# A single-core hybrid attention block: earlier weights for head 1, and low parts moved from GpSimd to VectorE

## The chip, the cores and the metric

The kernel runs on one core of a Trainium2 chip. The metric is the device time of one launch in microseconds (us). Three runs of the kernel before took 897.99, 901.11 and 902.21 us, with a median of 901.11 us. All times below come from one further execution, which the hardware profiler recorded.

## What is computed

One layer of a hybrid encoder block works on 1024 tokens of width 1024, in float32. The input is normed, multiplied by one wide matrix `w_in`, and the columns of the result go to a gated linear attention with four heads and to a short gated convolution. Both are gated, joined, and sent through `w_out`. The reference, cut to what matters here:

```python
h = rmsnorm(x, norm_g)                        # x * rsqrt(mean(x*x) + eps) * g
proj = jnp.einsum('bsd,de->bse', h, w_in)     # 1024 x 1024 by 1024 x 7200
q, k, v, z_a, lr_f, lr_b, b_gate, c_gate, h_c, z_c = split(proj)
o = gla(q, k, v, decay(lr_f)) + reversed_gla(q, k, v, decay(lr_b))
y_a = rmsnorm(o) * gla_norm_g * silu(z_a)
y_c = b_gate * conv3(c_gate * h_c) * silu(z_c)
out = rmsnorm(x + concat(y_a, y_c) @ w_out, final_g)
```

Only the columns of `v` and the preparation of `h` for the later columns are touched by the change.

## The kernel before, in words

**Split numbers.** TensorE multiplies in a reduced float32 format. Each operand is kept as two tiles: a high part `hi` (a cast of the number) and a low part `lo` (the number less its high part). A product is three matmuls, hi by hi, hi by lo and lo by hi. The helper `split` (L150 to L153) makes the two: ScalarE casts, and GpSimd subtracts unless another engine is named.

**The x stage (L214 to L265).** The eight tiles of 128 tokens are loaded, scaled by their root mean square and by `norm_g` (spread over the partitions into the tile `gb` by two matmuls), transposed on TensorE, and split into the blocks `hb`. Between these steps TensorE multiplies the tiles that are ready by the weights of head 0's values, one block `t` per tile. All of this is in an order written out by hand (`tc.manual_schedule`), and so is the next stage. Head 1's weights are loaded in block 4 and split after block 7, in whole tiles of 128x1024.

**The values of head 1 (L285 to L344).** `values(1, wv)` runs 192 matmuls in four steps. Beside each step, `sums` prepares a quarter of three sums of the blocks of `h`, called t1, t2 and t3. They are needed later, since a product of two 2x2 block matrices is made with seven block products instead of eight. Each sum is a subtraction on VectorE (L310) and a split: a cast on ScalarE (`t_hi`) and a subtraction on GpSimd (`t_lo`).

**The values of heads 2 and 3 (`value_pair`, L453).** Seven block products, each in two halves, with weights a00, a01, a10, a11 and sums of them. In the order of TensorE: o00, o01, os2 (with t2), os3 (with t3), os1 (with t1), o11 (with t4) and os4. VectorE adds each result from its PSUM bank (L483 to L502). Beside o01, os2 and os3 it runs the generator `later_sums`, which makes a fourth sum t4 and three sums of quarter blocks (tt1, tt2, tt3). Six banks (pa, pb, pc, twice each) are used in turn, so product 15 waits until VectorE has taken product 9 from its bank.

**The pairs of columns (`quad`, L544).** All further columns go through `second` (products of quarter blocks) and `pair` (products of blocks). The first `quad` begins where `value_pair` ends; its first bank is that of os1. `second` adds its second product to the first at L528, and TensorE then reuses that bank.

**What sets the order.** Each engine takes its own instructions in order, and engines wait for each other on semaphores. Where no order is written out, a scheduler places the instructions, and `issue_after` pins some of them. All loads and stores go through the one queue of the sync engine, also in order.

Of the kernel before, what the change touches and what calls it, by code (L numbers as in the profile page):

```python
# [37 lines left out]
def tile_hybrid_gla_shortconv(ctx, tc, x, norm_g, w_in, w_gk_f, b_gk_f, w_gk_b, b_gk_b,  # L38
# [66 lines left out]
    ident = const.tile([P, P], F32, name="ident")  # L105
    make_identity(nc, ident)
    ones = xp.tile([1, P], F32, name="ones")
    G.memset(ones, 1.0)
    mhalf = const.tile([P, 1], F32, name="mhalf")
    G.memset(mhalf, -0.5)  # L110
    smask = const.tile([P, 512], F32, name="smask")
# [62 lines left out]
    def scale_x(t, rs):  # L174
        for o in (0, 512):
            sl = slice(o, o + 512)
            V.scalar_tensor_tensor(xts[t][:, sl], xts[t][:, sl], rs, gb[:, sl], ALU.mult, ALU.mult)  # L177

    def turn_x(t):

        for d in range(2):
            ps = pq.tile([P, 512], F32, name=("pa", "pb", "pc")[(2 * t + d) % 3])
            for c in range(4):
                T.transpose(ps[:, c * P:(c + 1) * P], xts[t][:, (4 * d + c) * P:(4 * d + c + 1) * P], ident)
            hi, lo = (b[:, :, t % 4 * P:(t % 4 + 1) * P] for b in hb[d][t // 4])
# [4 lines left out]
    def h_tile(part, c, t):  # L190
        return hb[c // 4][t // 4][part][:, c % 4, t % 4 * P:(t % 4 + 1) * P]

    def split_v(raw, e_hi=A, e_lo=G):
        pr = tuple(vw.tile([P, 4, DV], F32R, name=f"v_{n}") for n in ("hi", "lo"))
        split(*pr, raw, e_hi, e_lo)
        return pr

    last_mm = [None]

# [13 lines left out]

    with tc.manual_schedule():  # L214

        gb = xp.tile([P, D], F32, name="gb")

        def spread_g(o, scaled):
            ps = bank()
            T.matmul(ps, ones, g_row[:, o:o + 512], start=True, stop=True)  # L220
            scaled(gb[:, o:o + 512], ps)

        spread_g(0, lambda dst, src: V.tensor_scalar(dst, src, D ** 0.5, None, ALU.mult))
        rs0 = scale_of(0)
        spread_g(512, lambda dst, src: A.activation(dst, src, AF.Copy, scale=D ** 0.5))
        scale_x(0, rs0)
# [10 lines left out]
        src = lr_w.rearrange("p c (d k) -> p c d k", d=2)  # L240

        def split_lr(r):
            split(lrw6[:, :, :, r, 0], lrw6[:, :, :, r, 1], src, V, G)

        for t in range(NT):
            ps = bank()[:, 0:DV]
            mul_v(ps, t, wv, 0)
            if t + 2 < NT:
                rs = scale_of(t + 2)
            if t == 0:  # L250
                mul_v(ps, t, wv, 1)
            if t + 1 < NT:
                turn_x(t + 1)
            if t + 2 < NT:
                scale_x(t + 2, rs)
            if t > 0:
                mul_v(ps, t, wv, 1)
            mul_v(ps, t, wv, 2)
            store_v(0, t, ps)
            if t == NT - 4:  # L260
                raws = [load_v(1, i) for i in range(2)]
            if t in (4, 5):
                split_lr(t - 4)
            if t == NT - 1:
                w_next = [split_v(r) for r in raws]  # L265
    wv = w_next
    gk_hi, gk_lo = (fl(a) for a in y_pair())
    split(gk_hi, gk_lo, gk, V, V)
# [25 lines left out]


    t1, t2, t3 = (block(tp, f"t{i}") for i in (1, 2, 3))
    raws = [load_v(h, i) for h in (2, 3) for i in range(2)]

    def f_tile():
        return gt.tile([P, 512], F32, name="f")  # L300
# [5 lines left out]

    done = []

    def minus(a, b_, blk, c, f):
        done.append(V.tensor_tensor(f, a, b_, ALU.subtract))  # L310
        split(blk[0][:, c], blk[1][:, c], f)

    def sums():
        for c in range(4):
            f01, f00, f11 = (joined(hb[d][s_], c) for d, s_ in ((0, 1), (0, 0), (1, 1)))
            minus(f01, f00, t1, c, f00)
            minus(f11, f01, t3, c, f01)
            minus(f11, f00, t2, c, f11)
# [5 lines left out]
    def less(f, x, y, blk):  # L324
        V.tensor_tensor(f, x, y, ALU.subtract)
        split(*blk, f)


    quarters = [tuple(a[:, 2 * d:2 * d + 2, 256 * s_:256 * s_ + 256] for a in hb[1][0])
# [4 lines left out]
    def part(src, e_lo=G, late=False):  # L334
        pool, name, bufs = (resp, "w", 2) if late else (ws, "a", 6)
        hi, lo = (pool.tile([P, 4, P], F32R, name=f"{name}_{i}", bufs=bufs) for i in ("hi", "lo"))
        hi, lo = (a[:, 0:src.shape[1]] for a in (hi, lo))
        split(hi, lo, src, A, e_lo)
        return hi, lo
# [6 lines left out]
    def halves(a):  # L346
        return [a[:, o:o + 4] for o in (0, 4)]

    def parts(a):
        return [part(x) for x in halves(a)]  # L350

    a00, a01, a10, a11 = (fl(r).rearrange("p (c e) -> p c e", e=P) for r in raws)
    o00, o01 = parts(a00), parts(a01)
# [99 lines left out]
    def value_pair(h0, h1, o00, o01, os2, a00, a01, a10, a11, s2, beside):  # L453
# [24 lines left out]
        x, w = [tmp(), tmp()], [None, None]  # L478
        for i, ps in mul(o00, b00):
            A.copy(x[i], ps)  # L480
        for i, ps in mul(o01, b10):
            c = tmp()
            V.tensor_tensor(c, ps, x[i], ALU.add)  # L483
            out_v(h0, 0, i, c)
            next(beside)
        for i, ps in mul(os2, t2):
            V.tensor_tensor(x[i], ps, x[i], ALU.add)
            next(beside)
        for i, ps in mul(os3, t3):
            w[i] = tmp()  # L490
            V.tensor_tensor(w[i], ps, x[i], ALU.add)
            next(beside)
        for i, ps in mul(os1, t1):
            c = tmp()
            V.tensor_tensor(c, ps, w[i], ALU.add)
# [148 lines left out]

    def later_sums():

        for c in range(4):
            f = joined(t2, c, tmp)
            minus(joined(hb[1][0], c, tmp), f, t4, c, f)
            yield  # L650
        f = [tmp().rearrange("p (c t) -> p c t", c=2) for _ in range(3)]
        for f_, i in zip(f, (0, 1, 3)):
            whole(f_, quarters[i])
        less(f[0], f[1], f[0], tt1)
        yield
        less(f[1], f[2], f[1], tt3)
        less(f[0], f[2], f[0], tt2)
        yield

    with tc.issue_after(last_mm[0].ins):  # L660
# [4 lines left out]
    less(f[0], f[1], f[0], quarters[1])  # L665
    h2 = quarters[0], tt1, tt2, tt3, quarters[2], quarters[3], quarters[1]

    for j in range(CW // P):
# [380 lines left out]
```

## Time and profile before

| quantity | value |
|---|---|
| median of three runs | 901.11 us (897.99 to 902.21) |
| profiled execution, whole | 903.29 us |
| its span, first to last instruction | 901.2 us |
| TensorE (PE) busy | 865.7 us, 96% |
| VectorE (DVE) busy | 713.4 us, 79% |
| GpSimd (POOL) busy | 448.2 us, 50% |
| ScalarE (ACT) busy | 393.7 us, 44% |
| mean granted TensorE clock | 0.986 of full speed |

The span is what the trace covers; the profiled execution's own time has 2.1 us around it. A busy share is an average over stages that differ much: VectorE is at 79% overall and at almost 100% in some stretches of the first 130 us. TensorE's granted clock is 1.00 (2.4 GHz) or 0.50 (1.2 GHz) at any moment; a value between is the mean of a window. In a timeline an instruction's bracket tells how long its engine stood idle before it, and which instruction released it.

### The profile page before, as it was taken

The page shows a single profiled execution, that of the slowest core. Times are in us where ns is not written, and L with a number is a line of the kernel's source. Part 1 is how long each engine was busy: PE and PEld are TensorE (multiplying, and loading weights), DVE is VectorE, ACT ScalarE, POOL GpSimd, SP SyncE. Part 2 cuts the span into 40 slices and gives each one's busy share as a digit, 9 for nine tenths or more (in the row PEclk, how much of TensorE's full clock was granted, in tenths as well). Part 3 has the DMA queues.
Part 4 walks back from the last instruction along what each step waited for, and adds up shares of the span by engine and source line. Part 5 has one row for each costly group of instructions (what it writes and reads, how often), then busy time and mean ns, then how long its engine had stood idle before and what let it go on. Part 6 is the DMA issues. An engine that isn't in the chain of part 4 may idle for free.

```text
span 901.2 us, 12971 instructions
## 1 busy us (share of the span) xinstructions
PE 865.7 (96%) x4452; PEld 725.2 (80%) x4452; DVE 713.4 (79%) x1283; ACT 393.7 (44%) x822; POOL 448.2 (50%) x391
## 2 busy tenths in 40 slices
PE   7999969999999999999999999999999999999996
PEld 6999958887887878787878888887878787888885
DVE  6879986888888888888888565666799989975754
ACT  5533233434445362635344342443365446542553
POOL 3368676757768576768665655520112212222231
PEclk9999969999999999999999999999999999999999
DMA  7521332222231313132233433468856344310122
GB/s 252 138 74 56 86 109 56 71 70 71 71 94 48 117 47 105 60 94 71 70 94 129 134 102 116 128 208 327 293 159 222 105 136 134 120 52 24 42 77 93
DMA packets 102163, 100.35 MB, mean 111 GB/s; under 512 B 10705, under 2 KB 82385, under 8 KB 101586
## 3 DMA queue, kind: packets, MB, share of 16 engines
q1 hardware_dynamic: 102098, 99.53, 35.0%
q8 instruction: 35, 0.57, 0.3%
q14 instruction: 30, 0.25, 0.1%
HBM read 71.20 MB, written 28.31 MB: 110 GB/s over the span
## 4 chain that ended last, share of the span: by engine, by line
PE 72%; DVE 17%; issue 4%; DMA 3%; POOL 2%; ACT 1%; SPq 0%; POOLq 0%; DVEq 0%; ACTq 0%
PE out L715 16%; PE pc L381 15%; PE pb L381 15%; PE pa L381 15%; PE po L872 3%; PE pu L917 2%; DVE tmp L304 1%; DVE tmp L635 1%; DVE tmp L430 1%; DVE f L304 1%; DMA k<-k_dram 1%; DVE s L407 1%; DMA raw<-in_w_in 1%; DVE xt L177 1%; DVE dd L820 1%
## 5 line engine op out<-in xcount | busy, mean ns | idle before, releaser
L153 POOL TENSOR_TENSOR a_lo<-s,a_hi 128x512 fp32r<-128x512 f32 x74 | 116.0, 1573 | 28.8 <-ACT a_hi L152 28.5
L153 POOL TENSOR_TENSOR a_lo<-tmp,a_hi 128x512 fp32r<-128x512 f32 x48 | 70.3, 1466 | 103.8 <-ACT a_hi L152 99.0
L153 POOL TENSOR_TENSOR a_lo<-raw,a_hi 128x512 fp32r<-128x512 f32 x84 | 111.2, 1327 | 14.8 <-ACT a_hi L152 14.8
L147 POOL TENSOR_TENSOR rs<-rs,mhalf 128x1 f32<-128x1 f32 x48 | 28.7, 598 | 142.6 <-DVE rs L146 135.2
L715 PE MATMUL out<-a_hi,y_hi 128*128 128x512 f32 x192 | 89.2, 465 | 0.5 <-ACT y_hi L152 0.5
L152 ACT CAST a_hi<-raw 128x512 fp32r<-128x512 f32 x108 | 63.8, 595 | 58.3 <-PE pc L381 17.2
L152 ACT CAST a_hi<-tmp 128x512 fp32r<-128x512 f32 x48 | 29.8, 621 | 122.8 <-DVE tmp L407 99.4
L715 PE MATMUL out<-a_hi,y_lo 128*128 128x512 f32 x192 | 77.1, 401 | 0.0
L715 PE MATMUL out<-a_lo,y_hi 128*128 128x512 f32 x192 | 77.0, 401 | 0.0
L827 POOL TENSOR_TENSOR kt<-kt,k 128x256 f32<-128x256 f32 x32 | 26.3, 821 | 97.7 <-ACT kt L824 70.8
L152 ACT CAST a_hi<-s 128x512 fp32r<-128x512 f32 x74 | 45.0, 617 | 47.4 <-PE pa L381 17.5
L381 PE MATMUL pa<-h_hi,a_hi 128*128 128x512 f32 (+1 forms) x128 | 47.7, 373 | 5.2 <-DVE tmp L528 2.8
L381 PE MATMUL pb<-h_hi,a_hi 128*128 128x512 f32 (+1 forms) x128 | 48.2, 376 | 4.5 <-DVE tmp L528 3.8
L381 PE MATMUL pc<-h_hi,a_hi 128*128 128x512 f32 (+1 forms) x128 | 48.0, 375 | 2.6 <-DVE tmp L528 2.6
L381 PE MATMUL pa<-h_hi,a_lo 128*128 128x512 f32 (+1 forms) x128 | 47.0, 367 | 0.7 <-POOL a_lo L153 0.7
L381 PE MATMUL pc<-h_lo,a_hi 128*128 128x512 f32 (+1 forms) x128 | 47.2, 369 | 0.0
L381 PE MATMUL pb<-h_hi,a_lo 128*128 128x512 f32 (+1 forms) x128 | 47.2, 369 | 0.0
L381 PE MATMUL pc<-h_hi,a_lo 128*128 128x512 f32 (+1 forms) x128 | 47.1, 368 | 0.0
L381 PE MATMUL pb<-h_lo,a_hi 128*128 128x512 f32 (+1 forms) x128 | 47.1, 368 | 0.0
L381 PE MATMUL pa<-h_lo,a_hi 128*128 128x512 f32 (+1 forms) x128 | 46.8, 365 | 0.0
L715 PEld LDWEIGHTS out<-a_hi,y_lo 128*128 128x128 f32 x192 | 36.4, 190 | 8.0
L717 DVE TENSOR_TENSOR res<-out,res 128x512 f32<-128x512 f32 x48 | 32.9, 686 | 12.4 <-PE out L715 12.3
(344 smaller groups left out, 2735.2 us busy)
## 6 DMA issues: line engine op xcount, KB each, us to landing
raw<-in_w_in SPq DMA_DIRECT2D x56, 512.0 KB, 4.0
raw<-in_w_out SPq DMA_DIRECT2D x16, 512.0 KB, 3.9
xt<-in_x SPq DMA_DIRECT2D x8, 512.0 KB, 8.4
yc_dram<-tmp SPq DMA_DIRECT2D x16, 256.0 KB, 2.0
b_dram<-u SPq DMA_DIRECT2D x8, 512.0 KB, 2.6
z_dram<-tmp SPq DMA_DIRECT2D x16, 256.0 KB, 2.4
s<-yc_dram SPq DMA_DIRECT2D x16, 256.0 KB, 3.9
raw<-in_x SPq DMA_DIRECT2D x8, 512.0 KB, 6.7
```

What stands on the lines that cost most here:

```text
L147: G.tensor_tensor(rs, rs, mhalf, ALU.pow)
L152: (e_hi.copy if e_hi is A else e_hi.tensor_copy)(hi, src)
L153: e_lo.tensor_tensor(lo, src, hi.bitcast(F32), ALU.subtract)
L177: V.scalar_tensor_tensor(xts[t][:, sl], xts[t][:, sl], rs, gb[:, sl], ALU.mult, ALU.mult)
L304: V.tensor_tensor(f, blk[0].bitcast(F32)[:, c], blk[1].bitcast(F32)[:, c], ALU.add)
L381: T.matmul(ps, a[x0][:, k], b_[x1][:, k], start=start and k == 0 and j == 0, stop=stop and k == n - 1 and j == 2, skip_group_check=not start)
L407: V.tensor_tensor(f, x0, x1, op)
L715: T.matmul(ps, a[:, j, :], w, start=j == 0 and i == 0, stop=j == 3 and i == 2)
L717: V.tensor_tensor(res[t][:, cs], ps, (xr if row0 == NT else res[t])[:, cs], ALU.add)
L827: G.tensor_tensor(kk, kk, k4, ALU.mult)
L872: T.matmul(o, l, m, start=j == 0, stop=j == len(mm) - 1)
L917: T.matmul(pu[:, d], ks[:, d], r["v"][:, t], start=True, stop=True)
```

## The change

- Head 1's two weight tiles are loaded directly behind the eight tiles of x, and are split in halves of 128x512 after blocks 5 and 6. The loads of a00 and a01 move up to block 1, those of a10 and a11 to block 6; o00 is split at block 7.
- `gb` stays in the PSUM tiles `pc`; the factor D ** 0.5 goes into the row of ones. The two copies of it are gone, and `turn_x` takes only the banks pa and pb.
- The low parts of t1, t2, t3 (12 subtractions), of t4 (4) and of tt1, tt2, tt3 (3) go from GpSimd to VectorE, and are written behind the next sum instead of at once. The last quarter (`quarters[1]`) keeps its split on GpSimd.
- `later_sums` gives t4 in two steps, beside the two halves of the first product, and its further steps beside the second.

```diff
+    v_raw1 = [load_v(1, i) for i in range(2)]      # behind load_x(2..7)
     ...
-    G.memset(ones, 1.0)
+    G.memset(ones, D ** 0.5)
     ...
-            V.scalar_tensor_tensor(xts[t][:, sl], xts[t][:, sl], rs, gb[:, sl], ALU.mult, ALU.mult)
+            V.scalar_tensor_tensor(xts[t][:, sl], xts[t][:, sl], rs, gb[o // 512], ALU.mult, ALU.mult)
     ...
-            ps = pq.tile([P, 512], F32, name=("pa", "pb", "pc")[(2 * t + d) % 3])
+            ps = pq.tile([P, 512], F32, name=("pa", "pb")[d])
     ...
-        split(*pr, raw, e_hi, e_lo)
+        for o in (0, 2):
+            split(*(a[:, o:o + 2] for a in (*pr, raw)))
     ...
+        gb = [pq.tile([P, 512], F32, name="pc") for _ in range(2)]
+        for i in range(2):
+            T.matmul(gb[i], ones, g_row[:, 512 * i:512 * i + 512], start=True, stop=True)
     ...
-            if t == NT - 4:
-                raws = [load_v(1, i) for i in range(2)]
+            if t == 1:
+                a00, a01 = (load_a(2, i) for i in range(2))
+            if t in (5, 6):
+                w_next.append(split_v(v_raw1[t - 5]))
+            if t == 6:
+                a10, a11 = (load_a(3, i) for i in range(2))
     ...
-            if t == NT - 1:
-                w_next = [split_v(r) for r in raws]
+            if t == 7:
+                o00 = parts(a00)
     ...
-    def minus(a, b_, blk, c, f):
+    def split_later(behind, hi, lo, f):
+
+        A.copy(hi, f)
+        for x in behind:
+            V.tensor_tensor(*x, ALU.subtract)
+        behind[:] = [(lo, f, hi.bitcast(F32))]
+
+    def finish_low(behind):
+        while behind:
+            V.tensor_tensor(*behind.pop(), ALU.subtract)
+
+    def minus(a, b_, blk, c, f, behind):
         done.append(V.tensor_tensor(f, a, b_, ALU.subtract))
-        split(blk[0][:, c], blk[1][:, c], f)
+        split_later(behind, blk[0][:, c], blk[1][:, c], f)
     ...
         for i, ps in mul(o00, b00):
             A.copy(x[i], ps)
+            next(beside)
         for i, ps in mul(o01, b10):
     ...
             next(beside)
         for i, ps in mul(os2, t2):
             V.tensor_tensor(x[i], ps, x[i], ALU.add)
-            next(beside)
         for i, ps in mul(os3, t3):
             w[i] = tmp()
             V.tensor_tensor(w[i], ps, x[i], ALU.add)
-            next(beside)
     ...
-            minus(joined(hb[1][0], c, tmp), f, t4, c, f)
-            yield
+            minus(joined(hb[1][0], c, tmp), f, t4, c, f, behind)
+            if c % 2 == 1:
+                yield
+        finish_low(behind)
     ...
-        less(f[0], f[1], f[0], tt1)
+        less(f[0], f[1], f[0], tt1, behind)
         yield
-        less(f[1], f[2], f[1], tt3)
-        less(f[0], f[2], f[0], tt2)
+        less(f[1], f[2], f[1], tt3, behind)
+        less(f[0], f[2], f[0], tt2, behind)
+        finish_low(behind)
         yield
```

The first place is VectorE beside the values of head 1, from the last tile of x on. `f` holds a sum of two parts (L304; L320 in the changed kernel) or a difference of two sums (L310; L337), `t_lo` is a low part, and the rows with `out` belong to the decay's low-rank input. Before:

```order
L304 TENSOR_TENSOR f<-h_hi,h_lo 128x512 x3
L310 TENSOR_TENSOR f<-f 128x512 x3
L304 TENSOR_TENSOR f<-h_hi,h_lo 128x512
L278 TENSOR_TENSOR y_hi<-out,y_hi 32x512 x2
L278 TENSOR_TENSOR y_lo<-out,y_lo 32x512 x2
L304 TENSOR_TENSOR f<-h_hi,h_lo 128x512 x2
L310 TENSOR_TENSOR f<-f 128x512 x3
L304 TENSOR_TENSOR f<-h_hi,h_lo 128x512
```

In the changed kernel the same place reads:

```order
L320 TENSOR_TENSOR f<-h_hi,h_lo 128x512 x3
L337 TENSOR_TENSOR f<-f 128x512 x2
L295 TENSOR_TENSOR y_hi<-out,y_hi 32x512 x2
L295 TENSOR_TENSOR y_lo<-out,y_lo 32x512 x2
L329 TENSOR_TENSOR t_lo<-f,t_hi 128x512
L337 TENSOR_TENSOR f<-f 128x512
L329 TENSOR_TENSOR t_lo<-f,t_hi 128x512
L334 TENSOR_TENSOR t_lo<-f,t_hi 128x512
L320 TENSOR_TENSOR f<-h_hi,h_lo 128x512 x3
L337 TENSOR_TENSOR f<-f 128x512 x2
```

Each quarter of the sums now has three more subtractions on VectorE, each behind the next difference, and the third directly behind the second.

The second place is GpSimd from the last block of the x stage on. `v_lo` is head 1's low part, `a_lo` that of the weights (from `raw` as loaded, or from their sums in `s`), `t_lo`, `h_lo`, `y_lo` and `tt_lo` those of t1 to t3, t4, tt1, and tt2 with tt3. Before:

```order
L153 TENSOR_TENSOR a_lo<-raw,a_hi 128x512 x4
L153 TENSOR_TENSOR v_lo<-raw,v_hi 128x1024 x2
L153 TENSOR_TENSOR t_lo<-f,t_hi 128x512 x12
L603 MEMSET u 128x1
L604 MEMSET u 128x1
L153 TENSOR_TENSOR a_lo<-s,a_hi 128x512 x2
L153 TENSOR_TENSOR a_lo<-raw,a_hi 128x512 x3
L153 TENSOR_TENSOR h_lo<-tmp,h_hi 128x512
...
L153 TENSOR_TENSOR a_lo<-raw,a_hi 128x512 x2
L153 TENSOR_TENSOR y_lo<-tmp,y_hi 128x512
L153 TENSOR_TENSOR tt_lo<-tmp,tt_hi 128x512 x2
```

In the changed kernel:

```order
L154 TENSOR_TENSOR v_lo<-raw,v_hi 128x512 x2
L154 TENSOR_TENSOR lrw<-lr_w,lrw 128x16x16
L154 TENSOR_TENSOR v_lo<-raw,v_hi 128x512 x2
L154 TENSOR_TENSOR a_lo<-raw,a_hi 128x512 x4
L617 MEMSET u 128x1
L618 MEMSET u 128x1
L154 TENSOR_TENSOR a_lo<-s,a_hi 128x512 x2
L154 TENSOR_TENSOR a_lo<-raw,a_hi 128x512 x8
L154 TENSOR_TENSOR h_lo<-r_1461,h_hi 128x2x256
```

The 12 rows of `t_lo` and the seven of `h_lo`, `y_lo` and `tt_lo` are gone from GpSimd, `v_lo` stands ahead of `a_lo`, and the eight `a_lo` of `value_pair` follow one another. From L528 of the first `quad` on, the order on every engine is the same in both kernels.

## Rows read from the trace of the kernel before

**Rows 1.** The page: busy time, share of the span and instructions by engine.
```profile
PE 865.7 (96%) x4452; PEld 725.2 (80%) x4452; DVE 713.4 (79%) x1283; ACT 393.7 (44%) x822; POOL 448.2 (50%) x391
```

**Rows 2.** Windows by stage; columns in the first line, PEclk is the granted clock.
```profile
core 0: us, PE busy (x) PEld busy (x) DVE busy (x) ACT busy (x) POOL busy (x), PEclk, DMA share, GB/s
0.00:20.00 20.00, 15.12 (x74) 11.22 (x75) 12.24 (x21) 10.05 (x17) 7.33 (x21) 1.00 0.78 282
72.10:100.40 28.30, 28.30 (x242) 28.30 (x242) 28.17 (x25) 9.65 (x17) 21.38 (x16) 1.00 0.24 66
100.40:113.30 12.90, 11.63 (x98) 11.03 (x96) 11.66 (x13) 2.91 (x5) 8.59 (x6) 1.00 0.31 81
113.30:128.50 15.20, 7.17 (x31) 6.17 (x30) 14.94 (x19) 5.31 (x11) 10.86 (x9) 0.66 0.28 105
128.50:134.00 5.50, 5.42 (x21) 4.52 (x22) 2.83 (x5) 1.48 (x4) 4.12 (x3) 0.69 0.43 101
134.00:901.20 767.20, 746.51 (x3584) 614.28 (x3582) 599.45 (x1151) 340.43 (x725) 367.68 (x317) 0.99 0.35 110
```

**Rows 3.** Waits of PE from 0 to 135: total us, times, longest.
```profile
PE pb L381 <- DVE tmp L497: 3.0, 1, 3.0
PE pa L381 <- DVE tmp L497: 2.2, 1, 2.2
PE pb L381 <- DVE tmp L528: 1.9, 1, 1.9
PE out L204 <- POOL v_lo L153: 0.4, 1, 0.4
PE pb L184 <- DVE xt L177: 0.3, 1, 0.3
PE out L274 <- ACT s L211: 0.2, 1, 0.2
```

**Rows 4.** Timeline of PE: start, us, line, operation.
```profile
72.15 0.28 PE L464 MATMUL pb<-a_hi,h_hi 128*128 128x256 f32 x1
113.03 0.28 PE L464 MATMUL pc<-a_lo,h_hi 128*128 128x256 f32 x1
128.58 0.38 PE L381 MATMUL pb<-h_hi,a_hi 128*128 128x256 f32 x1 [1.90 <-DVE tmp L528]
```

**Rows 5.** Timeline of DVE, the same columns.
```profile
38.20 1.89 DVE L304 TENSOR_TENSOR f<-h_hi,h_lo 128x512 f32<-128x512 f32 x3
49.69 1.39 DVE L278 TENSOR_TENSOR y_lo<-out,y_lo 32x512 fp32r<-32x512 f32 x2 [1.83 <-ACT y_lo L276]
76.33 3.48 DVE L359 TENSOR_TENSOR s<-raw 128x512 f32<-128x512 f32 x2
108.71 0.68 DVE L325 TENSOR_TENSOR tmp<-tmp 128x512 f32<-128x512 f32 x1
128.12 0.41 DVE L528 TENSOR_TENSOR tmp<-pb,tmp 128x256 f32<-128x256 f32 x1
```

**Rows 6.** Timeline of POOL, the same columns.
```profile
74.57 4.69 POOL L153 TENSOR_TENSOR t_lo<-f,t_hi 128x512 fp32r<-128x512 f32 x3 [2.49 <-ACT t_hi L152]
115.52 1.26 POOL L153 TENSOR_TENSOR a_lo<-raw,a_hi 128x512 fp32r<-128x512 f32 x1
116.74 1.72 POOL L153 TENSOR_TENSOR a_lo<-s,a_hi 128x512 fp32r<-128x512 f32 x1
```

**Rows 7.** Windows: one stretch of the port, with the columns of Rows 2.
```profile
72.70:128.46 55.76, 46.51 (x363) 44.90 (x361) 54.12 (x54) 17.83 (x33) 40.79 (x30) 0.91 0.27 81
```

**Rows 8.** Timeline of ACT, the same columns.
```profile
109.42 0.62 ACT L152 CAST y_hi<-tmp 128x512 fp32r<-128x512 f32 x1 [7.05 <-DVE tmp L325]
```

**Rows 9.** The DMA queue, its issues (count, KB, us to landing), and ACT there.
```profile
22.36 9.74 SPq L212 DMA_DIRECT2D v_dram<-s  x5
v_dram<-s SPq DMA_DIRECT2D x8, 128.0 KB, 2.0
27.71 0.37 ACT L211 COPY s<-out 128x256 f32<-128x256 f32 x1 [1.19 <-PE out L204]
```

More of the change, by code (lines that the diff above doesn't have):

```diff
@@ L191, in h_tile, with split_v, halves, parts @@
         return hb[c // 4][t // 4][part][:, c % 4, t % 4 * P:(t % 4 + 1) * P]
-    def split_v(raw, e_hi=A, e_lo=G):
+    def split_v(raw):
         pr = tuple(vw.tile([P, 4, DV], F32R, name=f"v_{n}") for n in ("hi", "lo"))
-        split(*pr, raw, e_hi, e_lo)
-        return pr
+        for o in (0, 2):
+            split(*(a[:, o:o + 2] for a in (*pr, raw)))
+        return pr
+    def halves(a):
+        return [a[:, o:o + 4] for o in (0, 4)]
+    def parts(a):
+        return [part(x) for x in halves(a)]
+    def part(src, e_lo=G, late=False):
+        pool, name, bufs = (resp, "w", 2) if late else (ws, "a", 6)
+        hi, lo = (pool.tile([P, 4, P], F32R, name=f"{name}_{i}", bufs=bufs) for i in ("hi", "lo"))
+        hi, lo = (a[:, 0:src.shape[1]] for a in (hi, lo))
+        split(hi, lo, src, A, e_lo)
+        return hi, lo
+    def load_a(h, i):
+        return fl(load_v(h, i)).rearrange("p (c e) -> p c e", e=P)
     last_mm = [None]
@@ L214, in tile_hybrid_gla_shortconv @@
     with tc.manual_schedule():
[L216 to L226, printed above, removed]
+        gb = [pq.tile([P, 512], F32, name="pc") for _ in range(2)]
+        for i in range(2):
+            T.matmul(gb[i], ones, g_row[:, 512 * i:512 * i + 512], start=True, stop=True)
+        scale_x(0, scale_of(0))
         rs1 = scale_of(1)
@@ L243, in split_lr @@
             split(lrw6[:, :, :, r, 0], lrw6[:, :, :, r, 1], src, V, G)
+        w_next = []
         for t in range(NT):
@@ L296, in tile_hybrid_gla_shortconv @@
     t1, t2, t3 = (block(tp, f"t{i}") for i in (1, 2, 3))
-    raws = [load_v(h, i) for h in (2, 3) for i in range(2)]
     def f_tile():
@@ L307, in tile_hybrid_gla_shortconv @@
     done = []
-    def minus(a, b_, blk, c, f):
+    def split_later(behind, hi, lo, f):
[7 more added lines that the diff above has]
+    def minus(a, b_, blk, c, f, behind):
         done.append(V.tensor_tensor(f, a, b_, ALU.subtract))
-        split(blk[0][:, c], blk[1][:, c], f)
+        split_later(behind, blk[0][:, c], blk[1][:, c], f)
     def sums():
+        behind = []
         for c in range(4):
             f01, f00, f11 = (joined(hb[d][s_], c) for d, s_ in ((0, 1), (0, 0), (1, 1)))
-            minus(f01, f00, t1, c, f00)
-            minus(f11, f01, t3, c, f01)
-            minus(f11, f00, t2, c, f11)
+            minus(f01, f00, t1, c, f00, behind)
+            minus(f11, f01, t3, c, f01, behind)
+            minus(f11, f00, t2, c, f11, behind)
+            finish_low(behind)
             yield
@@ L322, in whole, with less @@
         V.tensor_tensor(f, blk[0].bitcast(F32), blk[1].bitcast(F32), ALU.add)
-    def less(f, x, y, blk):
+    def less(f, x, y, blk, behind):
         V.tensor_tensor(f, x, y, ALU.subtract)
-        split(*blk, f)
+        split_later(behind, *blk, f)
     quarters = [tuple(a[:, 2 * d:2 * d + 2, 256 * s_:256 * s_ + 256] for a in hb[1][0])
@@ L332, in tile_hybrid_gla_shortconv @@
     tt2, tt3 = (tuple(tp.tile([P, 2, 256], F32R, name=f"tt{i}_{n}") for n in ("hi", "lo")) for i in (2, 3))
[L334 to L339, printed above, removed]
     beside = sums()
@@ L344, in tile_hybrid_gla_shortconv @@
             next(beside, None)
[L346 to L353, printed above, removed]
+    o01 = parts(a01)
     with tc.issue_after(done[5].ins):
@@ L645, in later_sums @@
     def later_sums():
+        behind = []
         for c in range(4):
             f = joined(t2, c, tmp)
-            minus(joined(hb[1][0], c, tmp), f, t4, c, f)
-            yield
+            minus(joined(hb[1][0], c, tmp), f, t4, c, f, behind)
+            if c % 2 == 1:
+                yield
+        finish_low(behind)
         f = [tmp().rearrange("p (c t) -> p c t", c=2) for _ in range(3)]
@@ L653, in later_sums @@
             whole(f_, quarters[i])
-        less(f[0], f[1], f[0], tt1)
+        less(f[0], f[1], f[0], tt1, behind)
         yield
-        less(f[1], f[2], f[1], tt3)
-        less(f[0], f[2], f[0], tt2)
+        less(f[1], f[2], f[1], tt3, behind)
+        less(f[0], f[2], f[0], tt2, behind)
+        finish_low(behind)
         yield
@@ L664, in tile_hybrid_gla_shortconv @@
     whole(f[1], quarters[2])
-    less(f[0], f[1], f[0], quarters[1])
+    V.tensor_tensor(f[0], f[1], f[0], ALU.subtract)
+    split(*quarters[1], f[0])
     h2 = quarters[0], tt1, tt2, tt3, quarters[2], quarters[3], quarters[1]
```

## The prediction, made before the changed kernel was run

> **What bounds the kernel now.** I read the page first: PE is busy for 865.7 of the span's 901.2 us [rows 1], so only PE's gaps can be won back. The windows by stage then say where they are [rows 2]. From 134 us on, PE is busy for 746.5 of 767.2 us at a mean clock of 0.99, and nothing that the change moves lies there. From 72.1 to 100.4 us PE is never idle. The gaps lie behind: 1.27 us (12.90 less 11.63) from 100.4 to 113.3, and 8.03 us (15.20 less 7.17) from 113.3 to 128.5, where the clock is also granted at 0.66 on average, so part of it ran at the lower level of 1.2 GHz. The window from 128.5 to 134 has no gap to speak of but a clock of 0.69: (1 - 0.69) x 2 x 5.5 = 3.4 us at the lower level, which cost 1.7 us of matmul time.
>
> The waits of PE name the releaser: VectorE at L497 twice (3.0 and 2.2 us) and at L528 (1.9 us) [rows 3]. These are instructions that take finished products out of PSUM. PE ended `value_pair` at about 113.1 us, and the first row behind L528 starts at 128.58 [rows 4]. VectorE is busy 54.1 of the 55.8 us ahead of that [rows 7], so it is VectorE that comes late, with a backlog that it collects far earlier.
>
> Why VectorE is slow there is read from single instructions. Three 128x512 subtractions or additions of SBUF tiles take 1.89 us when GpSimd is idle [rows 5], and successive ones start 0.60 us apart (a row shows 0.68 because the ends overlap). At 76.33 us, with GpSimd at work on its `t_lo` [rows 6], two take 3.48 us, or 1.74 each. GpSimd's own subtraction starts 1.22 us before the next when VectorE leaves it room [rows 6], and takes 4.69 us for three, 1.56 each, when it does not. 0.60 and 1.22 make 1.82, close to the 1.74: the two engines take turns, and each instruction of one waits for the whole of one of the other. I call what they share the port.
>
> This can be tested on a whole stretch. From 72.7 us to the end of L528 at 128.46, the window counts 54 instructions on VectorE and 30 on GpSimd [rows 7]. Two of VectorE's reach over the window's edges, and two of GpSimd's are memsets and one starts at the very end. Of VectorE's other 52, 15 take a PSUM operand, 33 are of 128x512 from SBUF alone and 4 of half that size. Of GpSimd's 27, one is of half size. In turns: 33 x 0.60 + 4 x 0.35 + 26 x 1.22 + 0.6 = 19.8 + 1.4 + 31.7 + 0.6 = 53.5 us. The stretch is 55.76 us, so 2.2 us is left for everything else. (0.35 is the 0.41 of L528 [rows 5] without its overlap.) The port bounds this stretch.
>
> **The change, part by part.**
>
> *Start.* The gb copies leave engines that wait for x. The pair of scalings beside GpSimd's first `v_lo` now reads one operand from PSUM, and PE's 0.3 us wait for xt [rows 3] should go. With head 1's split moved ahead, the waits for `v_lo` (0.4) and for the store copy `s` (0.2) go too. Together 0.9 us: PE begins `value_pair` at 71.3 instead of 72.15 [rows 4].
>
> The two loads add 1.05 MB ahead of 16 small ones on SP's queue; at the 282 GB/s of the first window [rows 2] that is 3.7 us. The first store of v then starts at 26.1 instead of 22.36 and lands 2.0 us later [rows 9], at 28.1, while the copy that takes its buffer again stood at 27.71. That is 0.4 us late on ScalarE, which had 1.19 us of room just before it [rows 9]. The small loads that VectorE reads at about 28 us come 3.7 us later and still in time. I cost this at nothing; without the cover it is 0.4 us, and at most the 0.9 us won above. GpSimd's splits of head 1 (4 halves, 4.9 us) go between its rare short tasks of the x stage.
>
> *Low parts of t1 to t3.* On VectorE this stretch opens behind the copy of the second low-rank half, which ends at 51.0 [rows 5] and, with PE 0.9 us ahead, at 50.1. From there to the end of the sums there are 12 low parts and 19 other instructions, and two of double length (a00 and a10): 35 units x 0.60 = 21.0 us, if GpSimd is silent. It is: from 38.2 us [rows 5] it has two halves of `v_lo`, a small one of 0.7 and four `a_lo`, 8.0 us, in turns with five VectorE instructions, 3.0 us, so until 49.2 at most; the next it has is the `a_lo` of s, behind the sums. A low part must wait for ScalarE's cast: 0.03 us behind the difference (109.39 to 109.42 [rows 5, 8]), 0.62 for the cast, 0.08 to the next engine, 0.73 in all. One instruction of 0.60 lies between, so 0.13 is left; about five low parts of the twelve meet it: 0.7 us. The sums end at 50.1 + 21.7 = 71.8 us, where before L359 started at 76.33 [rows 5].
>
> *The stretch behind it.* From 71.8 to L528's successor the port has on VectorE 37 full instructions (the 33 of before, less 3 differences now done, plus 4 low parts of t4 and 3 of tt1 to tt3) and 4 halves, on GpSimd 16 and one half (10 low parts are gone). In turns: 37 x 0.60 + 1.4 + 16 x 1.22 + 0.6 = 43.7 us. With the same 2.2 us left over, L528's successor ends at 71.8 + 45.9 = 117.7 instead of 128.46.
>
> What PE can do by itself: 113.1 less 0.9 less the 1.27 of gaps (its low parts of t4 come earlier) is 110.9, plus five products of 6 x 0.117 us, 114.4. So VectorE stays the later one by 3.3 us, and that remains as gaps. The gain is 128.46 - 117.7 = 10.8 us, and all behind it moves up by as much. The weights' low parts come close: ahead of the last `a_lo` of os4 the port has 30 instructions of VectorE and that is GpSimd's tenth, 18.0 + 12.2 us, so it ends near 102.0; PE wants os4 after twelve half products of 24 x 0.117 us, at 71.3 + 33.7 = 105.0.
>
> *Clock.* 3.3 us of gaps are more than the 1.9 us before the lower level in 128.5 to 134, but in smaller pieces. I keep that 1.7 us as spent; if the clock stays up, the time is 1.7 us shorter.
>
> *Sum.* 903.3 us, the profiled execution's own time, becomes 892.5. It stood 2.2 us above the median of the runs shown, 901.1, so against that: 890.3, or 890 us.
>
> *Bounds.* At best VectorE is in time everywhere: L528's successor at 114.4 + 0.35, a gain of 13.7, with 1.7 of the clock 15.4, which gives 885.7. At worst every one of the 19 low parts stands for one more cast of 0.62: 11.8 us, the whole gain, 902.1. I take the value near the best, since one instruction lies between nearly all.
>
> **The rivals.**
>
> *A. The low parts wait for ScalarE.* VectorE takes its instructions in order, so behind a low part that waits stand the PSUM results. ScalarE also copies o00's products and casts weights, in order, so a cast may stand behind one of these that waits for PE. For it: ScalarE was held 7.05 us before a cast of this kind [rows 8]. Against it: that wait was for VectorE itself, and ScalarE was busy for only 17.8 of 55.8 us [rows 7]. All 19 at 0.62 give 902; half of them 896.
>
> *B. Nothing is won by changing the engine.* An instruction that holds the port holds it on either engine; were it as long on VectorE as on GpSimd, the sum of 53.5 us would stay and only the 0.9 us at the start remain: 900.2. Against it stand 0.60 and 1.22 us for the same shape. The Trainium skill, "Perfetto Trace Analysis", section "Optimizing Scalar/DVE Operations", warns of just this: since the two share a port, moving work between them might not help. The trace agrees that they shut each other out, but not that the price is the same.
>
> *C. VectorE becomes the bound, and the kernel slower.* The 1.74 us may be VectorE's own pace in this stretch and not a turn with GpSimd. Then the 19 added instructions cost 1.74 each, 19 x (1.74 - 0.60) = 21.7 us more than in my sum: 912. The point from which the change loses is 0.60 + 10.8 / 19 = 1.17 us each. For it: VectorE is never idle from 72.1 to 100.4 (28.17 of 28.30 us [rows 2]). Against it: the 1.89 us for three [rows 5] of the same code.
>
> *D. It doesn't do what it says:* the loads behind x do not land in time for the split in block 5. The fourth copy of a block stands at 27.71 [rows 9], the split two blocks later; the loads come ahead of stores that start near 26. I leave this in the 0.9 us of the start.
>
> **How the numbers follow.** The forecast, with the clock either way and an error of 4 us on the late stretch, gets 0.80; A 0.12, B 0.04, C 0.04. Half a per cent, 4.5 us, is about what a measurement of this kernel can tell from no change. Faster by more than that is the forecast and the milder part of A, 0.85; within it the rest of A and B, 0.11; slower C, 0.04. The range goes from just under the best case, 885, to 897, where (897 - 890.3) / 0.62, or 11 of the 19 low parts, stand for one cast; B, C and the worse half of A lie above, some 0.13.
>
> **What would show it.** In the changed profile: VectorE's 128x512 sums at 0.6 us from about 50 to 72 us, with GpSimd silent; its `s` of a11 less a00 near 72 and not 76; `value_pair` on PE without a gap up to about 111; no wait over 2 us behind it; PE's first row behind L528's successor near 118. If low parts show idle time before them released by ScalarE, of more than 3 us in all, A is at work; if VectorE's sums take 1.7 us while GpSimd is idle, C is; if the windows behind 134 us change by more than 3 us of PE's gaps, I have missed what the shift does to the first `quad`.

## The result, and the profile after

The changed kernel took 890.57 us (median of four runs, 889.61 to 892.51), the kernel before 900.58 us beside it (four runs, 897.99 to 902.21): a ratio of 0.9889 with a 95% interval of 0.9870 to 0.9909. Its profiled execution took 889.61 us, with a span of 887.9 us. The same kernel on another chip took 892.95 us (ratio 0.9898, 0.9882 to 0.9914).

First the page of the changed kernel, busy time by engine, which answers to [rows 1]:

```profile
PE 860.0 (97%) x4452; PEld 722.8 (81%) x4452; DVE 704.4 (79%) x1301; ACT 393.7 (44%) x823; POOL 421.6 (47%) x374
```

Of the 13.3 us by which the span is shorter, 7.6 are idle time of PE (901.2 - 865.7 before, 887.9 - 860.0 now) and 5.7 are matmul time: the same 4452 matmuls, with less of the time at the lower clock (the mean granted clock is 0.995 instead of 0.986). The windows by stage of the changed kernel, with the columns of [rows 2], say where:

```profile
71.00:99.30 28.30, 28.30 (x243) 28.30 (x242) 28.15 (x35) 11.77 (x22) 14.04 (x9) 1.00 0.23 66
99.30:111.00 11.70, 11.70 (x102) 11.69 (x100) 11.70 (x16) 3.20 (x7) 8.88 (x7) 1.00 0.36 90
111.00:118.00 7.00, 4.42 (x32) 3.71 (x30) 7.00 (x11) 0.97 (x3) 3.22 (x4) 1.00 0.48 177
118.00:123.00 5.00, 4.11 (x15) 3.62 (x16) 3.64 (x6) 2.03 (x4) 4.24 (x3) 0.66 0.61 177
123.00:134.00 11.00, 11.00 (x53) 9.16 (x52) 4.31 (x8) 2.25 (x4) 3.85 (x3) 1.00 0.18 48
134.00:887.90 753.90, 733.94 (x3538) 604.53 (x3536) 594.31 (x1144) 338.55 (x721) 364.05 (x314) 1.00 0.35 111
```

`value_pair` now runs without a gap to 111 us. The 9.3 us of gaps behind it have become 3.5 (2.58 and 0.89), and a stretch of (1 - 0.66) x 2 x 5.0 = 3.4 us at 1.2 GHz is still there. The waits of PE from 0 to 135 us, against [rows 3], and PE's timeline, against [rows 4]:

```profile
PE pb L396 <- DVE tmp L542: 2.3, 1, 2.3
PE pc L396 <- ACT a_hi L153: 0.9, 1, 0.9
PE out L223 <- DVE v_hi L242: 0.6, 1, 0.6
PE pb L396 <- DVE tmp L511: 0.3, 1, 0.3
```

```profile
71.46 0.28 PE L479 MATMUL pb<-a_hi,h_hi 128*128 128x256 f32 x1
118.89 0.58 PE L396 MATMUL pb<-h_hi,a_hi 128*128 128x256 f32 x1 [2.32 <-DVE tmp L542]
```

L542 is L528's successor and L511 is L497's. Of the two waits of 3.0 and 2.2 us for L497, 0.3 us is left, and the work behind the third wait starts at 118.89 instead of 128.58: 9.7 us. Then VectorE's timeline, against [rows 5], and GpSimd's, against [rows 6]:

```profile
51.09 0.69 DVE L329 TENSOR_TENSOR t_lo<-f,t_hi 128x512 fp32r<-128x512 f32 x1
51.70 0.69 DVE L337 TENSOR_TENSOR f<-f 128x512 f32<-128x512 f32 x1
52.30 0.69 DVE L329 TENSOR_TENSOR t_lo<-f,t_hi 128x512 fp32r<-128x512 f32 x1
53.07 0.69 DVE L334 TENSOR_TENSOR t_lo<-f,t_hi 128x512 fp32r<-128x512 f32 x1
72.92 1.28 DVE L374 TENSOR_TENSOR s<-raw 128x512 f32<-128x512 f32 x2
76.43 1.78 DVE L320 TENSOR_TENSOR tmp<-t_hi,t_lo 128x512 f32<-128x512 f32 x1
118.43 0.41 DVE L542 TENSOR_TENSOR tmp<-pb,tmp 128x256 f32<-128x256 f32 x1
```

```profile
74.34 3.32 POOL L154 TENSOR_TENSOR a_lo<-s,a_hi 128x512 fp32r<-128x512 f32 x2 [24.84 <-ACT a_hi L153]
95.43 6.81 POOL L154 TENSOR_TENSOR a_lo<-raw,a_hi 128x512 fp32r<-128x512 f32 x4 [4.22 <-ACT a_hi L153]
```

While GpSimd is silent (24.84 us of idle time before 74.34), nearly every sum and low part of VectorE starts 0.60 us after the one before it (0.77 from 52.30 to 53.07, where a low part stands for its cast). As soon as GpSimd works again, a row takes 1.78 (76.43). The two additions of `s` that took 3.48 us now take 1.28 and start 3.4 us earlier.

The other 3.6 us of the span (772.6 us from the first row behind L528 to the end before, 769.0 behind L542 now) are 2.9 us of matmul time (751.93 against 749.05 us for the same 3602 matmuls) and 0.7 us of idle time. The matmul time is clock. Windows of before, then of the changed kernel, around the same two places of the program (9.7 us earlier, and 11.4 with the first loss):

```profile
286.00:302.00 16.00, 14.43 (x74) 12.05 (x74) 12.33 (x19) 10.02 (x16) 13.28 (x12) 0.89 0.31 89
618.00:630.00 12.00, 9.99 (x39) 7.77 (x39) 9.68 (x29) 5.70 (x17) 1.72 (x2) 0.86 0.82 316
```

```profile
276.30:292.30 16.00, 14.53 (x82) 12.29 (x82) 13.93 (x20) 9.97 (x16) 13.38 (x13) 1.00 0.33 94
606.60:618.60 12.00, 10.86 (x50) 8.41 (x49) 11.09 (x35) 5.78 (x17) 1.72 (x2) 1.00 1.00 378
```

A granted 0.89 over 16 us and 0.86 over 12 are 3.4 to 3.5 us each at the lower level, which cost up to 1.7 us of matmul time apiece (less where PE idled meanwhile); there were two such places and now none. The first looks alike otherwise (PE idle for 1.57 and 1.47 us). Among the profiles of the experiments, some have a lower clock at one of these places and others at neither, so I count this part to the two executions and not to the change: the medians differ by 10.0 us, the two profiled executions by 13.7.

### The profile page after: what moved, and what is told of

Its sections match the earlier page's. It is cut to its first block, busy times and chain, and to the rows that moved or that the text cites. A ratio compares the mean times of both kernels' runs of the same rounds, so it can differ in the third digit from the quotient of the medians.

```text
span 887.9 us, 12975 instructions
## 1 busy us (share of the span) xinstructions
PE 860.0 (97%) x4452; PEld 722.8 (81%) x4452; DVE 704.4 (79%) x1301; ACT 393.7 (44%) x823; POOL 421.6 (47%) x374
## 4 chain that ended last, share of the span: by engine, by line
PE 76%; DVE 17%; issue 3%; DMA 2%; ACT 1%; SPq 0%; POOLq 0%; POOL 0%; DVEq 0%; ACTq 0%
PE out L734 16%; PE pa L396 16%; PE pb L396 15%; PE pc L396 15%; PE po L891 4%; PE out L223 3%; PE pu L936 2%; DVE tmp L445 1%; DVE tmp L649 1%; DVE s L422 1%; DVE tmp L320 1%; DMA b<-b_dram 1%; PE out L291 1%; DMA xt<-in_x 1%; PE pk L928 1%
```

## The experiments

All are edits of the changed kernel; ratios are against the kernel before, run beside each.

**Which engine does the low parts.** All 19 go back to GpSimd, still one operation late:

```diff
         for x in behind:
-            V.tensor_tensor(*x, ALU.subtract)
+            G.tensor_tensor(*x, ALU.subtract)
...
         while behind:
-            V.tensor_tensor(*behind.pop(), ALU.subtract)
+            G.tensor_tensor(*behind.pop(), ALU.subtract)
```

> The changed kernel with all 19 low parts of t1 to t4 and tt1 to tt3 on GpSimd again, in the same places. Theory (the two engines take turns at a port, 0.60 us for VectorE, 1.22 for GpSimd): the port's sum grows by 19 x 0.62 = 11.8 us, nearly all of it late on VectorE; only the 0.7 us at the start stays: 898 to 901 us, ratio 0.998 to 1.002 of before. Rival (the gain comes from head 1's early weights and the new order of the sums): 890 to 892.

Measured: 899.70 us, ratio 0.9970 (0.9955 to 0.9985). The gain all but goes with the engine, so rival B falls. VectorE's timeline of this kernel, then PE's waits from 76 to 140 us:

```profile
78.40 3.47 DVE L374 TENSOR_TENSOR s<-raw 128x512 f32<-128x512 f32 x2
```

```profile
PE pa L479 <- POOL a_lo L154: 3.5, 2, 2.4
PE pc L479 <- POOL a_lo L154: 2.3, 2, 1.6
```

`s` takes 3.47 us again, 1.74 each, and starts 5.5 us later than in the changed kernel. Most of that is this execution's own late start (`value_pair` at 76.26 instead of 71.46; 3.7 of these 4.8 us were there already at the low-rank matmuls, at 45.28 instead of 41.58). The loss is behind the sums: from `value_pair`'s start to L542 it is 53.2 us (129.47 - 76.26) instead of 47.0, and PE waits for weights' low parts that GpSimd now does later. This profile is of the slowest of the ten runs; of the 9.1 us between the medians it shows 6.2 at this place.

**The order.** Each low part stands directly behind its own difference, on VectorE:

```diff
         A.copy(hi, f)
-        for x in behind:
-            V.tensor_tensor(*x, ALU.subtract)
-        behind[:] = [(lo, f, hi.bitcast(F32))]
+        V.tensor_tensor(lo, f, hi.bitcast(F32), ALU.subtract)
```

> The changed kernel with each low part written directly behind its own difference, on VectorE still. Theory: a low part is ready 0.73 us after its difference (0.03, the cast's 0.62, 0.08), so with nothing between VectorE stands idle up to 0.73 us at each, instead of 0.13: 11 of the 12 in the sums of t1 to t3, 6 to 8 us, so the sums end near 80 instead of 73.0. Behind it GpSimd uses part of such time for its own turns. Total 895 to 899. Rival (the wait for the cast is hidden by something else, the place behind the next difference is worth nothing): 890 to 892.

Measured: 901.51 us, ratio 1.0000 (0.9978 to 1.0022): the order is worth as much as the engine, more than I expected. VectorE's timeline and PE's waits of this kernel:

```profile
53.09 0.69 DVE L328 TENSOR_TENSOR t_lo<-f,t_hi 128x512 fp32r<-128x512 f32 x1 [0.82 <-ACT t_hi L327]
55.07 0.69 DVE L328 TENSOR_TENSOR t_lo<-f,t_hi 128x512 fp32r<-128x512 f32 x1 [0.69 <-ACT t_hi L327]
```

```profile
PE pa L477 <- DVE tmp L497: 3.2, 1, 3.2
PE pb L394 <- DVE tmp L540: 3.0, 1, 3.0
PE pb L477 <- DVE tmp L497: 1.3, 1, 1.3
PE pb L394 <- POOL a_lo L154: 1.2, 1, 1.2
```

Eight of the twelve low parts stand 0.7 to 0.8 us for ScalarE's cast (expected were eleven). The second `s` starts at 79.64 us (73.5 in the changed kernel) and the late stretch loses a little more: L540 (the same instruction as L542) is at 126.12, 7.7 us later. PE then waits 8.7 us between 71 and 140 in four pieces, and the mean clock of the execution is 0.991 where the changed kernel had 0.995. This is rival A, made real. That its upper end of 902 was met is partly luck: it stands for a shift of 11.8 us at L542, of which the trace shows 7.7; the rest of the 10.9 us between the medians lies elsewhere.

**The low parts of t4 and tt alone.** Seven go back to GpSimd, the twelve of t1 to t3 stay:

```diff
-    def split_later(behind, hi, lo, f):
+    def split_later(behind, hi, lo, f, e=V):
...
-        split_later(behind, *blk, f)
+        split_later(behind, *blk, f, G)
...
-            minus(joined(hb[1][0], c, tmp), f, t4, c, f, behind)
+            minus(joined(hb[1][0], c, tmp), f, t4, c, f, behind, G)
```

> The seven low parts of t4 and of the tt pairs are on GpSimd; the twelve of t1 to t3 stay on VectorE. My theory (turns at the port, 1.22 us of GpSimd against 0.60 of VectorE for a subtraction): the sums end at 72.9 us as in the changed kernel, but the stretch behind them gets 7 x 0.62 = 4.3 us longer, so L542 starts near 122.7 instead of 118.4 and the time is 894 to 896 us. Rival (the gain comes from the sums alone, because VectorE was the late engine there; behind them only PE counts): L542 stays within 1 us of 118.4 and the time at 890 to 892 us.

Measured: 894.34 us, ratio 0.9908 (0.9879 to 0.9938). VectorE's timeline:

```profile
122.67 0.41 DVE L542 TENSOR_TENSOR tmp<-pb,tmp 128x256 f32<-128x256 f32 x1
```

From the start of `value_pair` (72.19 here, 71.46 in the changed kernel) to L542 it is 50.5 us instead of 47.0: 3.5 us for seven moved instructions, 0.50 each where I had 0.62. The time agrees with that. The sums alone are not the whole gain.

**Turns, tested directly.** Twelve more instructions on GpSimd that nothing waits for, beside the sums:

```diff
             finish_low(behind)
+            if c == 0:
+                V.tensor_tensor(smask, smask, smask, ALU.mult)
+                for _ in range(12):
+                    G.tensor_tensor(smask, smask, smask, ALU.mult)
```

> In addition to the changed kernel's work, twelve multiplications of a 128x512 tile with itself (a mask of ones and zeros, so its values stay) run on GpSimd beside the sums of t1 to t3, released by one such instruction on VectorE at about 53.7 us. Nothing waits for them but GpSimd's next own work at 74.3 us. My theory (turns): each of the twelve holds a VectorE instruction up by 1.22 us, VectorE's sums show 1.7 to 1.8 us each while the twelve run, and the sums end at 72.9 + 0.6 + 12 x 1.22 = 88.1 us; the time is 902 to 908 us. Rival C (the 1.74 us were VectorE's own pace behind the sums): VectorE's rows stay at 0.60 to 0.69, the sums end at 73.5 and the time is 890 to 892.5 us.

Measured: 900.17 us, ratio 0.9978 (0.9957 to 0.9998). VectorE's timeline, then GpSimd's:

```profile
59.80 2.97 DVE L337 TENSOR_TENSOR f<-f 128x512 f32<-128x512 f32 x2
62.69 1.52 DVE L329 TENSOR_TENSOR t_lo<-f,t_hi 128x512 fp32r<-128x512 f32 x1
74.81 0.68 DVE L337 TENSOR_TENSOR f<-f 128x512 f32<-128x512 f32 x1
85.32 0.69 DVE L334 TENSOR_TENSOR t_lo<-f,t_hi 128x512 fp32r<-128x512 f32 x1
```

```profile
56.45 17.88 POOL L351 TENSOR_TENSOR smask<-smask 128x512 f32<-128x512 f32 x12 [5.04 <-DVE smask L349]
```

As long as the twelve run, the same sums take 1.5 us each; the first one behind them takes 0.68 again. That settles rival C: the slow pace is GpSimd's doing. The size was off, and the time lies below the 902 to 908 us expected: the sums take 9.8 us longer than without the twelve, 0.82 each and not 1.22. (From the first low part at 53.10 to the end of the last one's turn at 85.92 it is 32.8 us, less 0.6 for the added VectorE instruction and 0.6 for an `s` that now stands ahead of the last low part; in the changed kernel it is 21.8.) Whether a multiplication of a tile with itself holds the port for less time than a subtraction of two tiles was not tried.

The same with twenty-four instructions that only write:

```diff
-                for _ in range(12):
-                    G.tensor_tensor(smask, smask, smask, ALU.mult)
+                for _ in range(24):
+                    G.memset(smask.rearrange("p (c t) -> p c t", t=CH)[:, :, 1:CH], 1.0)
```

> As the kernel with twelve multiplications, but with twenty-four memsets on GpSimd (nearly all of a 128x512 tile, some 0.5 us each: instructions that only write). If every access of GpSimd to SBUF takes a turn, VectorE's sums show about 0.60 + 0.5 = 1.1 us each while the memsets run, and end at 73.5 + 24 x 0.5 = 85.5 us; time 900 to 905 us. If only instructions that read take turns, which is what the Trainium skill states, VectorE's rows stay at 0.60 to 0.69 us, the sums end near 73.5 and the time is 890 to 892.5 us. I hold the second for likelier, since the mask memsets of the kernel before gave no row that tells.

Measured: 890.89 us, ratio 0.9875 (0.9837 to 0.9912; two runs). VectorE's timeline, then GpSimd's:

```profile
58.69 0.69 DVE L329 TENSOR_TENSOR t_lo<-f,t_hi 128x512 fp32r<-128x512 f32 x1
59.30 0.69 DVE L337 TENSOR_TENSOR f<-f 128x512 f32<-128x512 f32 x1
```

```profile
55.65 13.83 POOL L351 MEMSET smask<- 128x504 f32 x24 [5.02 <-DVE smask L349]
```

GpSimd is busy too, and VectorE keeps its 0.60 us. The Trainium skill, "SBUF — State Buffer", section "Who interferes with whom", states both halves: a VectorE instruction with two SBUF inputs contends with a GpSimd instruction that reads SBUF, not with one that only writes it. The trace agrees, with 1.52 us for a row of L329 beside the multiplications and 0.69 us beside the memsets.

**The other parts of the change.** The x stage of before, with all else as in the changed kernel (the core of the edit):

```diff
-    v_raw1 = [load_v(1, i) for i in range(2)]
...
-            if t in (5, 6):
-                w_next.append(split_v(v_raw1[t - 5]))
...
+            if t == NT - 4:
+                raws = [load_v(1, i) for i in range(2)]
```

> The changed kernel with the x stage of before: gb copied, three banks for the transposes, head 1's weights loaded in block 4 and split whole after block 7, a00 to a11 loaded behind it. Theory: the start was worth 0.7 us at the first product of value_pair, and GpSimd's old split of head 1 ends near 52 us, so a few turns of the sums are lost to it, up to 2 us: 891 to 893.5. Rival (the early weights are half of the change's gain or more): 896 or more.

Measured: 891.77 us, ratio 0.9874 (0.9849 to 0.9900), the same as the changed kernel within the intervals: the new x stage is not where the gain comes from. And t4's sums at their old steps, behind the results of later products instead of the first two:

```diff
             A.copy(x[i], ps)
-            next(beside)
...
             V.tensor_tensor(x[i], ps, x[i], ALU.add)
+            next(beside)
```

> The changed kernel with the steps of t4's and the quarter sums where they were: one step behind each half of o01, os2 and os3, instead of all of t4 beside o00. Theory: VectorE now meets o01's first result in its queue near 76.5 us, and PE ends it at 79.9, so it stands 3 to 3.5 us; the port's sum is the same, so L542's successor comes later by what GpSimd can't use of that: 891.5 to 894. Rival (the moved steps don't matter): 890 to 891.

Measured: 895.44 us (890.92 to 897.40), ratio 0.9912 (0.9878 to 0.9946): higher than expected, with an interval that overlaps the changed kernel's. Its profile is of the fastest of its runs. VectorE's timeline:

```profile
80.51 0.69 DVE L498 TENSOR_TENSOR tmp<-pa,tmp 128x512 f32<-128x512 f32 x1 [3.71 <-PE pa L479]
```

VectorE is idle for 3.7 us, waiting for PE at a result that now stands ahead of t4's sums, and L542's counterpart starts at 120.30, 48.5 us behind `value_pair`'s start (71.76) instead of 47.0. So 1.6 us of the 4.9 are shown; the rest is open.

**What is left: a PSUM bank.** In each quad a product had to wait until L542 had emptied its bank; it gets a fifth:

```diff
-        bx, by, bz, bw = (bank6()[:, lo] for _ in range(4))
+        bx, by, bz, bw, bv = (bank6()[:, lo] for _ in range(5))
...
-        product(by, o3, t4, True, True)
-        V.tensor_tensor(r[1][:, lo], by, u, ALU.add)
+        product(bv, o3, t4, True, True)
+        V.tensor_tensor(r[1][:, lo], bv, u, ALU.add)
```

> In the quads the product with t4 gets a fifth PSUM bank instead of the one that L542 has to empty first; nothing else is changed. My theory (VectorE is still the later engine at L542, and PE waits there for the bank alone): the wait of 2.3 us at L542 goes and a part of it, up to 1.5 us, returns as a wait for the next bank that VectorE has not emptied; over the later quads 7.3 us of such waits go or are halved. Time 882 to 888 us. Rival (VectorE is in order, and the next result behind L542 waits just as long): the waits move to the next bank in full and the time is 889.5 to 891.5 us.

Measured: 888.80 us, ratio 0.9850 (0.9826 to 0.9873), between the two expectations. Then, on top of it, the product with t4 ahead of the one that adds to the first bank:

```diff
-        product(bx, last_(o0), b10, False, True)
-        A.copy(r[0][:, lo], bx)
         product(bv, o3, t4, True, True)
         V.tensor_tensor(r[1][:, lo], bv, u, ALU.add)
+        product(bx, last_(o0), b10, False, True)
+        A.copy(r[0][:, lo], bx)
```

> The kernel with a fifth bank, and in each quad the product with t4 now stands ahead of the one that adds to the first bank (which has to wait until ScalarE's L540 has copied that bank out). In the profile of the kernel with the fifth bank PE waited seven times for L540, 6.3 us in all, 0.9 us each. My theory: each wait shortens by the product moved ahead of it, 6 x 0.117 = 0.7 us, so some 4.9 us go; time 883 to 886 us. Rival (the wait is for ScalarE's place in its own order, and PE only comes to the next wait earlier: for VectorE's results or for the weights): the time stays at 888 to 890 us.

Measured: 888.63 us, ratio 0.9854 (0.9834 to 0.9873). PE's waits behind 140 us, of the changed kernel, with the fifth bank, and with bank and order:

```profile
PE pa L396 <- DVE tmp L542: 2.8, 3, 1.0
PE pc L396 <- DVE tmp L542: 2.6, 3, 1.0
PE pb L396 <- DVE tmp L542: 1.9, 2, 1.0
```

```profile
PE pc L396 <- ACT tmp L540: 2.6, 2, 1.7
PE pb L396 <- ACT tmp L540: 1.9, 3, 0.9
PE pa L396 <- ACT tmp L540: 1.8, 2, 0.9
```

```profile
PE pb L396 <- DVE r L546: 2.2, 3, 0.8
PE pa L396 <- DVE r L546: 1.7, 2, 0.9
PE pc L396 <- DVE r L546: 1.6, 2, 0.8
```

The waits move: 7.3 us for L542, then 6.3 for L540, then 5.5 for L546. My theory expected most of them gone and was wrong twice; the rival, that PE comes earlier to the next late result, is what the rows show: each edit leaves 0.8 to 1.0 us less of them. Beside the kernel with bank and order the changed kernel ran on the same chip:

> The changed kernel itself, beside the kernel with the other bank and order on the same chip, to tell how far its profile varies between executions: 889.5 to 892.5 us; a wait of 2 to 2.5 us at L542 and a start of VectorE's work on the low-rank rows (L295) anywhere from 49.5 to 52.5 us, as it stood in the profiles so far.

Measured: 892.95 us (891.91 to 894.75), a little above the range I expected. Bank and order (887.72 to 891.00) lie 4.3 us lower there. This second profile of the changed kernel also showed L295, the last instruction before the sums, at 51.54, and why. ScalarE's timeline of the first profile, then of the second:

```profile
28.15 0.37 ACT L230 COPY s<-out 128x256 f32<-128x256 f32 x1 [1.20 <-PE out L223]
```

```profile
30.16 0.37 ACT L230 COPY s<-out 128x256 f32<-128x256 f32 x1 [3.32 <-DMA v_dram<-s]
```

The copy waits for the store that has its buffer. This wait, of 2.2 to 5.4 us, is in nine profiles of kernels with the new start (the expectation below says eight; it is nine), and in neither of the two with the old one. The copy itself comes at 28.16 to 30.49 there, so the wait delays it by 0 to 2.3 us. It was removed with buffers:

```diff
-        vt = fl(ws.tile([P, 4, P], F32, name="s", bufs=3))[:, 0:n * DV]
+        vt = (xp.tile([P, DV], F32, name="sv", bufs=6) if h == 0 and n == 1
+              else fl(ws.tile([P, 4, P], F32, name="s", bufs=3))[:, 0:n * DV])
```

> The changed kernel with six buffers of their own for the copies of head 0's v that are stored in the x stage, instead of three shared ones. In eight profiles of the new start ScalarE's L230 waited 2.2 to 5.4 us for a store of v (only the first profile of the changed kernel shows no such wait), and value_pair began at 71.3 to 76.3 us, later with a longer wait. My theory (the loads of head 1's weights push the stores back by more than I allowed, and that eats the start's gain): no wait for a store at L230, value_pair near 71.2 us, and a time 1 to 2.5 us below the changed kernel's 890.6 and 893.0 us: 889 to 891 us. Rival (that wait is hidden, and the start of value_pair varies for another reason): value_pair still varies from 71.3 to 74 us and the time stays at 890.5 to 893 us.

Measured: 890.29 us (888.70 to 893.30), ratio 0.9890 (0.9862 to 0.9917). ScalarE's timeline:

```profile
28.04 0.37 ACT L231 COPY sv<-out 128x256 f32<-128x256 f32 x1 [1.19 <-PE out L223]
```

No store is waited for, and `value_pair` starts at 71.48, in both kernels with these buffers within 0.1 us; in the nine it starts at 71.34 to 76.26. That is later than the 71.2 I expected: the stores explain the spread, but not why the start wins nothing even without them (below). In the time alone the effect can't be told from none. All three together:

> The six store buffers, the fifth PSUM bank in the quads and the other order of the quads' last products together. If the terms add: 888.7 us of the kernel with bank and order, less the 1 to 2.5 us of the buffers: 886 to 888 us. If the buffers win nothing: 888 to 889.5 us.

Measured: 886.10 us (884.63 to 887.79), ratio 0.9833 (0.9808 to 0.9858): the fastest, 4.5 us below the first measurement of the changed kernel and 6.9 below the second, and in the range expected if the terms add. That they add is not shown: the buffers took 2.5 us off the kernel with bank and order and only 0.3 off the changed kernel, and both differences are as small as the spread of the runs.

## Why the prediction was right

**Start, 0.9 us: wrong.** `value_pair` started 0.7 us earlier (71.46), but VectorE's sums did not start at 50.1: L295 stood at 49.67, as before at 49.69 [rows 5], and the first low part came at 51.09. The step that failed is "with PE 0.9 us ahead, at 50.1". PE's rows, two of before and one of the changed kernel, show it:

```profile
41.50 0.47 PE L274 MATMUL out<-h_hi,lrw 128*128 128x512 f32 x1 [0.18 <-ACT s L211]
51.79 0.74 PE L204 MATMUL out<-v_lo,h_hi 128*128 128x256 f32 x4 [0.40 <-POOL v_lo L153]
```

```profile
41.58 0.39 PE L291 MATMUL out<-h_hi,lrw 128*128 128x512 f32 x1
```

The wait of 0.4 us for `v_lo` lay behind the low-rank matmuls (41.50 to 48.9) whose result the sums follow, so its end could not bring the sums forward. The waits of 0.3 and 0.2 us ahead of them did go, yet PE comes to these matmuls no earlier, at 41.58: it was already 0.4 us late at its fourth pair of transposes (21.63, before 21.20). No store is waited for in this profile, nor in that of the six store buffers, where the same matmul starts at 41.60. With the old start and all else changed it starts at 41.02, and `value_pair` at 71.01. So this part of the change won nothing; which piece of it costs PE these 0.4 us in the first 22 is not shown.

In most executions a second loss comes on top, from a step that I costed at nothing: "0.4 us late on ScalarE, which had 1.19 us of room" became waits of 2.2 to 5.4 us in nine profiles out of ten without the extra buffers. The landing of 2.0 us that I took from [rows 9] was that of a queue with less ahead of it: the median from issue to landing was 2.5 us in the first profile of the changed kernel and 3.4 in the second, and 2.1 with the old start.

**Low parts of t1 to t3, 21.7 us: right.** From 51.09 to 72.92 it took 21.8 us. In three of the four quarters the third low part starts 0.77 instead of 0.60 us behind the second (52.30 to 53.07), and in two the first one comes 0.18 late: five times, 0.9 us together, where I had counted five and 0.7 us.

**The stretch behind, 45.9 us: right.** From 72.92 to L542's end at 118.84 it took 45.9 us. The sum in turns holds here, where VectorE's partner subtracts two tiles. The gaps left on PE are 3.5 us (3.3 predicted), of which 0.9 is a wait for a cast on ScalarE that I had not counted and the rest waits for VectorE. os4's low part ended at 102.2 (102.0).

**Clock.** I kept the 1.7 us behind L542, and the stretch at the lower level was there. I did not foresee that the two other stretches at the lower level could be missing.

So the shift was 9.7 us and not 10.8, since the start brought VectorE's sums nothing. That the forecast of 890.3 met 890.57 so closely is partly luck. Between the medians the gain is 10.0 us, 0.8 less than forecast, and the kernel before took 900.58 us beside the changed one, 0.5 less than the 901.1 I had subtracted from: two errors of opposite sign. On the other chip the same kernel took 892.95.

**The rivals.** A falls for the order that was chosen and holds for the other one. B falls: by [rows 5, 6] the price of an instruction on the port depends on the engine, and 899.7 against 890.6 us shows it. C falls: in these runs VectorE slows only while GpSimd reads. D: the loads landed in time; what they displaced did not.

## What to carry to other kernels

Where VectorE and GpSimd both work on SBUF operands, add up both engines' time on the port; an instruction is worth moving to the engine that holds it for less, even if that engine is the busier one, but only with something between it and the cast it depends on. A wait removed at a bank that is shared in order came back here, for the most part, at the next one, so ask for the next late result before counting the gain. Loads put ahead of stores on one queue also made the stores land later here (a median of 2.5 to 3.8 us instead of 2.0), and the buffers behind them need that room.

## What was not expected of the hardware

GpSimd's multiplications (12 in 17.88 us) cost VectorE 0.82 us each where I expected 1.22; its memsets (24 in 13.83 us) cost nothing, which I held for likelier. `value_pair` of the same program started at 71.46 in one execution and at 73.34 in another, by when a store landed. And one place where PE idled for about 1.5 us in both profiles had the lower clock in the one and the full clock in the other.
